# Token-major gates, output products and feed-forward blocks in a two-block layer kernel on one Trainium2 core

## The chip, the cores and the metric

The kernel runs on one core of a Trainium2 chip. The metric is the device time of one execution, in microseconds (us); a profile of one execution gives the span of the instructions beside it. Engines are named as in the profile: PE is TensorE's matmul stream, PEld its weight loads, DVE VectorE, ACT ScalarE, POOL GpSimd, SP SyncE, which issues most of the transfers.

## What is computed

Two transformer blocks, one after the other, over 256 tokens of 2048 features, all in float32. Cut to the products:

```
# block 1
mod = silu(c) @ w_ada + b_ada            # sh_m, sc_m, gt_m, sh_f, sc_f, gt_f
h = rmsnorm(x, g[0]) * (1 + sc_m) + sh_m
q, k, v, g_ret, u, gate_r, gate_s = split(h @ w_in)
y_ret = (silu(g_ret) * head_group_norm(retention(rope(q), rope(k), v))) @ w_ret_out
glu_a, glu_b = split(gelu(s5_ssm(u, ...)) @ w_s5_glu)
merged = sigmoid(gate_r) * y_ret + sigmoid(gate_s) * (glu_a * sigmoid(glu_b))
x = x + gt_m * rmsnorm(merged @ w_out, g[1])
h = rmsnorm(x, g[2]) * (1 + sc_f) + sh_f
a, b = split(h @ w_ffn_in)               # 5632 columns each
x = x + gt_f * rmsnorm((silu(a) * b) @ w_ffn_out, g[3])
# block 2
proj = rms_norm(x, norm1_w) @ w_in_2     # q k v of two attentions, conv, three merge gates
mixed = sum(sigmoid(merge_n) * (branch_n @ w_br_n) for n in 3 branches)
x = x + mixed @ w_out_2
h2 = rms_norm(x, norm2_w)
x = x + (silu(h2 @ w_ffn_gate) * (h2 @ w_ffn_up)) @ w_ffn_down
out = rms_norm(x, final_norm_w)
```

## The kernel before

**Products.** A float32 product is made of three matmuls on halves: a weight page `raw` is split into `whi` (ScalarE) and `wlo` (VectorE), an activation into a high and a low page (`hh` and `hl`, `h2h` and `h2l`, and so on), and high x high, high x low and low x high are summed in one PSUM bank. There are two forms. `gemm` (line 361) keeps a 128x128 block of weights in TensorE and moves the 256 tokens (`mm3`): the result is feature-major, features on the partitions and tokens in the row, as the next product wants its input. `gemm_tok` (line 405) keeps 128 tokens in TensorE and moves 512 columns of the weights: the result is token-major, in two banks, one for each 128 tokens. Before the change `gemm_tok` makes the values `v` and the inner gate `g_ret` of block 1 and three products of block 2; all others use `gemm`.

**The order of the work.** Products are cut into halves (`Half`): one half is 1024 weight columns of 128 rows, 24 matmuls of 256 columns or 12 of 512. `run` goes through the halves in order: it loads pages ahead on SP's queue, splits the weights of a later half (`prepare`), emits the matmuls of the present one, then its `post` (the evictions), then `pump`. Work beside the products is written as Python generators (tasks): attention, the S5 part, gating. A `yield` gives control back; its letter and number say when the task may go on: "P" from a time on TensorE's planned clock, "A" or "V" when that engine is free, with a wait in planned us. `can` and `pump` (lines 255 to 300) decide by planned costs (`Times`, `Engine`). `self.later` holds low-half subtractions that are issued a step later, by `flush`. `split_page` (435) makes an activation's two halves, the second through `later`.

**Block 1, up to its first norm.** Six passes over `w_in` (`PASSES`, `GROUPS`, line 538 on) make partial sums while the input arrives; `REST` finishes them. The gates `gate_r` and `gate_s` go through a sigmoid to DRAM (`gate_done`, 1102) and come back as `gl` pages. `ret_done` (1242) multiplies the retention branch by its gate, `glu_a` and `glu_b` (1255 to 1280) the S5 branch, with the sum split for the output product. `s5_setup` (577) makes S5's constants on GpSimd with three functions on ScalarE. `ada` sums the modulation vectors `mods` on VectorE between the weight splits; the feature-major form holds them as one column for each 128 features.

**Norms.** The output product's results are feature-major, so `y_done` (1286) and `add_done` (1753) square pages and add them up, and TensorE sums over the partitions with a column of ones (`token_sums`, `folded_sums`). `double_norm` (1313) makes two norms from three such sums and `single_norm` one; `to_columns` spreads 1/rms over the partitions by a matmul, and `keep_warm` puts matmuls of ones in between. `modulated` (492) then makes the next product's input page by page. `ffn` (1388) is used for both feed-forward blocks: pairs of gate and up blocks, `gate_up` with silu x up, and the output product through `out_gemm`.

Of the kernel before, what the change touches and what calls it, by code (L numbers as in the profile page):

```python
# [153 lines left out]
class Core:  # L154
# [250 lines left out]
    def gemm_tok(self, name, col, xs, done, kts=KT, k0=0, sums=None):  # L405

        state = []

        def emit(ks):
            def f(hi, lo):  # L410
                if not state:
                    state.extend([self.mm_bank(), self.mm_bank()])
                for n, k in enumerate(ks):
                    xh, xl = xs(k)
                    wh, wl = hi[:, 512 * n:512 * n + 512], lo[:, 512 * n:512 * n + 512]
                    for t in range(2):
                        s = slice(128 * t, 128 * t + 128)
                        mm = self.PE.matmul
                        mm(state[t], xh[:, s], wh, start=k == k0 and not sums, stop=False, skip_group_check=True)
                        mm(state[t], xl[:, s], wh, start=False, stop=False, skip_group_check=True)  # L420
                        mm(state[t], xh[:, s], wl, start=False, stop=k == kts - 1, skip_group_check=True)
            return f

        def early():
            state.extend([self.mm_bank(), self.mm_bank()])
            for b, p in zip(state, sums()):
                self.A.activation(b, p, AF.Copy)

        for k in range(k0, kts, 2):
            ks = range(k, min(k + 2, kts))  # L430
            spec = [(name, 128 * kk, slice(col, col + 512)) for kk in ks]
            post = (lambda: done(state[0], state[1])) if k + 2 >= kts else None
            self.items.append(Half(spec, emit(ks), post, early=early if sums and k == k0 else None))
# [19 lines left out]

    def folded_sums(self, accs):

        st = self.sd_bank()
        for n, acc in enumerate(accs):
            self.V.tensor_add(acc[:, :256], acc[:, :256], acc[:, 256:])
            self.token_sums(st[:, 2 * n:2 * n + 2], acc[:, :256], n == 0)
        return st  # L460

    def out_gemm(self, name, xs, done, sums, before, kts=KT, each=None):

        for i in range(8):
            c = [cols(256 * i), cols(256 * i + 128)]
            if i < 7:
                self.gemm(name, [c], xs, done(i), kts, lambda i=i: before(i))
            else:
                self.gemm(name, [c[:1], c[1:]], xs, lambda b, ps: done(7, b)(b, ps), kts, lambda: before(7), each, ends=sums)
# [22 lines left out]
    def modulated(self, x, r, A, B, name, after=None):  # L492
# [3 lines left out]
        def make(k):  # L496
# [7 lines left out]
            if after:  # L504
                after(k)
            if B is None:
                self.A.activation(hi, t, AF.Copy)
            else:
                self.A.activation(hi, t, AF.Identity, bias=B(k))

            def rest():
                if B is None:
                    self.V.tensor_sub(lo, t, hi.bitcast(F32))
                else:
                    self.V.scalar_tensor_tensor(lo, t, B(k), hi.bitcast(F32), OP.add, OP.subtract)
                done.add(k)
            self.later.append(rest)
        self_made, done = [], set()

        def more():  # L520
            make(len(self_made))
            self_made.append(1)

        def get(k):
            while len(self_made) <= min(k + (2 if k else 1), KT - 1):
                more()
# [5 lines left out]
        get.more = more  # L532
        get.make = make
        get.pairs = pairs
        get.made = self_made
# [10 lines left out]
SPLIT = 2.3  # L546
SPREAD1 = (0.0, 1.0)
# [20 lines left out]
def program(K):  # L568
# [8 lines left out]
    def s5_setup():  # L577
# [48 lines left out]
        yield "A", 0.0  # L626
# [31 lines left out]
        V.tensor_add(den, t[0], t[1])  # L658
        K.V.reciprocal(den, den)
# [112 lines left out]
    late2 = [(5, k) for k in range(16)]  # L772

    def spread(lst, a, b):
# [5 lines left out]
        for n, it in enumerate(new):  # L780
            while n % 2 == 0 and at and at[0] <= n // 2:
                at.pop(0)
                ada(*lst.pop(0))
            K.items.append(it)
# [273 lines left out]
    two = lambda c: [cols(c), cols(c + 128)]  # L1058

    def item(what, i):  # L1060
        if what == "v":
            return slice(V0 + 512 * i, V0 + 512 * i + 512)
        return {"s": lambda: two(GS0 + 256 * i), "u": lambda: two(U0 + 256 * i), "q": lambda: rope_cols(Q0, i), "k": lambda: rope_cols(K0, i),
                "r": lambda: two(GR0 + 256 * i)}[what]()
# [11 lines left out]
    def ready(it, src):  # L1076
# [13 lines left out]
        elif what in "rs":  # L1090
            gate_done("rs".index(what), i)(0, src[0])
# [10 lines left out]
    def gate_done(which, i):  # L1102
        def f(b, ps):
            p = K.page("gate")
            A.activation(p, ps, AF.Sigmoid)
            K.G.dma_start(gsp[8 * which + i], p)
# [8 lines left out]
    def one_pass(group, k0, k1, more, then=None):  # L1115
# [3 lines left out]
        def emit(k, its):  # L1119
            def f(hi, lo):  # L1120
                if not banks:
                    held.extend(K.sd_bank() for _ in range(8 - MM))
                    pool = [K.mm_bank() for _ in range(MM)] + held
                    for what, i in group:
                        banks[what, i] = [pool.pop(0) for _ in range(2 if what == "v" else 1)]
                xh, xl = h(k)
                at = 0
                for it in its:
                    if it[0] == "v":
# [26 lines left out]
        for k in range(k0, k1):  # L1156
            for n in range(2):
                its, w = [], 0
                for it in group:
                    size = 512 if it[0] == "v" else 256  # L1160
# [41 lines left out]
    for g, k0 in REST:  # L1202
        for it in groups[g]:
            if it[0] == "v":
                K.gemm_tok("w_in", V0 + 512 * it[1], h, lambda a, b, it=it: ready(it, [a, b]), k0=k0, sums=lambda it=it: added(it))
# [4 lines left out]
    def g_done(hp):  # L1210
        def f(a, b):
            tg = [K.page("tg"), K.page("tg")]
            for t, p in enumerate((a, b)):
# [5 lines left out]
    for n in range(16):  # L1219
        if ("rs"[n // 8], n % 8) not in planned:  # L1220
            K.gemm("w_in", [two(GR0 + 256 * n)], h, gate_done(n // 8, n % 8))
    for hp in range(4):
        K.gemm_tok("w_in", R0_ + 512 * hp, h, g_done(hp))
# [9 lines left out]
    def ret_before(i):  # L1233
        def f():
            if i == 0:
# [3 lines left out]
            gate_load(i + 1)  # L1239
        return f  # L1240

    def ret_done(i):
        def f(b, ps):
            merged[i] = gl.pop(i)
            V.tensor_mul(merged[i], ps, merged[i])
        return f
    xrf = lambda k: K.halves_of(xr)(k)
    for i in range(8):
        K.gemm("w_ret_out", [[cols(256 * i), cols(256 * i + 128)]], xrf, ret_done(i), before=ret_before(i))


    mg = {}

    def glu_before(i):
        def f():
            if i == 0:
                K.finish(G["s5"])
                K.finish(G["ys"])
            gate_load(8 + i)
            gate_load(9 + i)  # L1260
        return f
    hold = {}

    def glu_a(i):
        def f(b, ps):
            hold[i] = ps
        return f

    def glu_b(i):
        def f(b, ps):  # L1270
            sg = K.page("sg")
            A.activation(sg, ps, AF.Sigmoid)
            V.tensor_mul(sg, hold.pop(i), sg)
            V.tensor_mul(sg, sg, gl.pop(8 + i))
            V.tensor_add(sg, sg, merged.pop(i))
            mg[i] = K.split_page(sg, "mg")
        return f
    ysf = lambda k: K.halves_of(ys)(k)
    for i in range(8):
        K.gemm("w_s5_glu", [[cols(256 * i), cols(256 * i + 128)]], ysf, glu_a(i), kts=8, before=glu_before(i))  # L1280
        K.gemm("w_s5_glu", [[cols(D + 256 * i), cols(D + 256 * i + 128)]], ysf, glu_b(i), kts=8)


    up = {}

    def y_done(i, mod, last, half=None):
        w = slice(0, 512) if half is None else slice(256 * half, 256 * half + 256)

        def f(b, ps):
            u = up[i] = up.get(i) or K.page("u")  # L1290
            x = G["xl"][i]
            if i == 0:
                G["acc"] = new = [K.page("acc") for _ in range(3)]
            else:
                new = [K.page("sq") for _ in range(3)]
            sy, sx, su = new
            A.activation(sy[:, w], ps[:, :w.stop - w.start], AF.Square)
            for j in range(2) if half is None else [half]:
                s = slice(256 * j, 256 * j + 256)
                A.activation(u[:, s], ps[:, s.start - w.start:s.stop - w.start], AF.Copy, scale=mods[:, 16 * mod + 2 * i + j:][:, :1])  # L1300
            A.activation(su[:, w], u[:, w], AF.Square)
            V.tensor_mul(sx[:, w], x[:, w], u[:, w])
            if half == 1:
                last([p[:, w] for p in new])
            elif i:
                for acc, p in zip(G["acc"], new):
                    V.tensor_add(acc[:, w], acc[:, w], p[:, w])
        return f

    def y_sums():  # L1310
        G["st"] = K.folded_sums(G.pop("acc"))

    def double_norm(A_, B_, dst, name, new):

        st = G.pop("st")
        st2 = K.sd_bank()
        for n, sq in enumerate(new):
# [627 lines left out]
```

## Time and profile before

| | |
|---|---|
| median of 3 runs | 3415.16 us (3412.63 to 3415.56) |
| the profiled execution: time | 3421.82 us |
| the profiled execution: span | 3420.0 us |
| granted TensorE clock, mean | 0.995 |
| weight and other data read from HBM | 716.32 MB, 214 GB/s over the span |
| weight splits, ScalarE and VectorE | 1,124 each, of 128x1024 |

A busy time of the page is the sum over an engine's instructions, and a share of it is of the span. A line of the timeline gives the start of an instruction and how long its record lasts; matmuls are pipelined, so the time that one costs is the distance from its start to the next start (its pitch), and not the length of its record. "[0.53 <-DVE wlo]" means that the engine stood idle for 0.53 us before and that the tile `wlo`, written by VectorE, released it. Nearly every instruction has line 150, a helper that records all operations, so instructions are told apart by the names of their tiles.

### The profile page before, as it was taken

Reading aid. Unit: us, or ns where it says so; the run is one execution under the profiler, and the core shown is the slowest. Engines: PE = TensorE matmul, PEld = TensorE weight load, DVE = VectorE, ACT = ScalarE, POOL = GpSimd, SP = SyncE. Lnnn points to the kernel's source line nnn. Section 1 sums busy time; section 2 is a strip of 40 time slices with the busy share of each in tenths; the row PEclk is TensorE's granted clock in tenths of the full one; section 3 lists DMA queues with packets and bytes.
Section 4 is the critical chain, followed back from the end, with each engine's and each line's share of the span. In section 5 each row is a group of like instructions: output and inputs, shape, how many; then the busy total and the mean of one; then the engine's idle time right before and its main releaser. Section 6 shows DMA issues by size and latency. Waiting matters only on the chain.

```text
span 3420.0 us, 63152 instructions
## 1 busy us (share of the span) xinstructions
PE 3378.1 (99%) x27336; PEld 3291.6 (96%) x27336; DVE 2038.9 (60%) x2376; ACT 1542.6 (45%) x1906; POOL 171.3 (5%) x309
## 2 busy tenths in 40 slices
PE   8899999999999999999999999999999999999999
PEld 7889998999999999999988999999999999999998
DVE  7787889778765555445555455444555644444444
ACT  4456555444444444444455444433444444444343
POOL 3401221000000000000000000000000000000000
PEclk9999999999999999999999999999999999999999
DMA  8786777788665665555554444555555545455543
GB/s 330 288 307 245 254 254 265 282 304 313 229 227 214 219 237 216 200 191 190 192 195 177 175 172 178 189 181 185 185 201 193 193 177 186 184 178 195 204 181 118
DMA packets 118745, 735.76 MB, mean 215 GB/s; under 512 B 15345, under 2 KB 18945, under 8 KB 34369
## 3 DMA queue, kind: packets, MB, share of 16 engines
q1 hardware_dynamic: 110050, 716.19, 57.5%
q0 software_dynamic: 7840, 14.48, 1.3%
q8 instruction: 214, 3.51, 0.4%
q10 hardware_dynamic: 576, 1.05, 0.1%
q14 instruction: 65, 0.53, 0.0%
HBM read 716.32 MB, written 14.68 MB: 214 GB/s over the span
## 4 chain that ended last, share of the span: by engine, by line
PE 93%; DVE 2%; DMA 2%; POOL 1%; ACT 1%; issue 0%; SPq 0%; DVEq 0%; ACTq 0%
PE mmb L150 89%; PE sdb L150 4%; POOL s5x L150 1%; DMA raw<-ws 1%; DVE raw L150 1%; DVE wlo L150 1%; ACT whi L150 0%; DMA s5x<-s5p 0%; DMA xl<-xT 0%; DMA s5b<-s5bc 0%; DVE xl L150 0%; ACT part L150 0%; DVE mt L150 0%; DVE part L150 0%; DVE rt L150 0%
## 5 line engine op out<-in xcount | busy, mean ns | idle before, releaser
L150 DVE TENSOR_TENSOR wlo<-raw,whi 128x1024 fp32r<-128x1024 f32 x1124 | 1358.9, 1222 | 654.9 <-ACT whi L150 652.1
L150 ACT ACTIVATE whi<-raw 128x1024 fp32r<-128x1024 f32 x1124 | 1178.4, 1057 | 1238.6 <-PE mmb L150 1089.2
L150 PE MATMUL mmb<-hh,whi 128*128 128x256 f32 x2148 | 612.5, 285 | 1.2 <-ACT part L150 1.1
L150 PE MATMUL mmb<-hl,whi 128*128 128x256 f32 x2148 | 609.0, 284 | 0.0
L150 PE MATMUL mmb<-hh,wlo 128*128 128x256 f32 x2148 | 608.8, 283 | 0.0
L150 PE MATMUL mmb<-h3h,whi 128*128 128x256 f32 x1552 | 442.3, 285 | 1.0 <-ACT h3h L150 1.0
L150 PE MATMUL mmb<-h3l,whi 128*128 128x256 f32 x1552 | 439.4, 283 | 0.3 <-DVE h3l L150 0.2
L150 PE MATMUL mmb<-h3h,wlo 128*128 128x256 f32 x1552 | 439.2, 283 | 0.0
L150 PEld LDWEIGHTS mmb<-hh,whi 128*128 128x128 f32 x2148 | 413.6, 193 | 5.0 <-ACT part L150 1.3
L150 PEld LDWEIGHTS mmb<-hl,whi 128*128 128x128 f32 x2148 | 413.6, 193 | 1.2
L150 PEld LDWEIGHTS mmb<-hh,wlo 128*128 128x128 f32 x2148 | 413.3, 192 | 0.0
L150 PE MATMUL mmb<-h2h,whi 128*128 128x256 f32 x1408 | 398.6, 283 | 1.1 <-ACT h2h L150 1.1
L150 PE MATMUL mmb<-h2l,whi 128*128 128x256 f32 x1408 | 398.7, 283 | 0.5 <-DVE h2l L150 0.4
L150 PE MATMUL mmb<-h4l,whi 128*128 128x256 f32 x1408 | 398.6, 283 | 0.1
L150 PE MATMUL mmb<-h4h,whi 128*128 128x256 f32 x1408 | 398.6, 283 | 0.0
L150 PE MATMUL mmb<-h4h,wlo 128*128 128x256 f32 x1408 | 398.5, 283 | 0.0
L150 PE MATMUL mmb<-h2h,wlo 128*128 128x256 f32 x1408 | 398.5, 283 | 0.0
L150 PEld LDWEIGHTS mmb<-h3h,whi 128*128 128x128 f32 x1552 | 297.8, 192 | 3.2 <-issue 1.4
L150 PEld LDWEIGHTS mmb<-h3l,whi 128*128 128x128 f32 x1552 | 297.9, 192 | 0.9 <-DVE h3l L150 0.7
L150 PEld LDWEIGHTS mmb<-h3h,wlo 128*128 128x128 f32 x1552 | 297.8, 192 | 0.0
L150 PEld LDWEIGHTS mmb<-h2h,whi 128*128 128x128 f32 x1408 | 270.3, 192 | 1.3 <-ACT h2h L150 1.3
L150 PEld LDWEIGHTS mmb<-h2l,whi 128*128 128x128 f32 x1408 | 270.3, 192 | 0.9 <-DVE h2l L150 0.9
(324 smaller groups left out, 5788.0 us busy)
## 6 DMA issues: line engine op xcount, KB each, us to landing
raw<-ws SPq DMA_DIRECT2D x657, 1024.0 KB, 4.9
gsp<-gate POOLq DMA_DIRECT2D x16, 256.0 KB, 4.6
gl<-gsp SPq DMA_DIRECT2D x16, 256.0 KB, 7.3
xl<-x1d SPq DMA_DIRECT2D x16, 256.0 KB, 6.4
x<-xT SPq DMA_DIRECT2D x8, 256.0 KB, 6.4
xl<-xT SPq DMA_DIRECT2D x8, 256.0 KB, 9.1
x1d<-u POOLq DMA_DIRECT2D x8, 256.0 KB, 2.5
x2d<-u POOLq DMA_DIRECT2D x8, 256.0 KB, 2.6
```

The costliest lines, as they stand in the source:

```text
L150: return f(*args, **kw)
```

## The change

Gates, the retention, S5 and branch outputs, the output projections, and both feed-forward blocks now use `gemm_tok`: tokens stationary, 512 weight columns moving. What follows each of them is token-major:

- `untok` (new) turns a token-major pair of pages back: per half page four 128x128 transposes on TensorE into a free bank, then `split_page` from the bank. `turned` makes the next product finish that task before it reads the page.
- `gate_done`, `ret_done`, `glu_b`, `glu_a`, `merge_done`, `br_done`, `gate`/`gate_up` work on two pages of 128 tokens x 512 features.
- The sums of the norms come from `accum_out` of the squaring instruction, in [128, 1] columns; `reduce_sum` adds the four. `token_sums` in the stream, `folded_sums` and `to_columns` leave these norms. `TAIL` = 30 and 16 matmuls of ones are put in front of a norm. `normed` (new) scales the pages per token, turns them with transposes and applies gain and shift per feature on the way out of the bank.
- Gains that vary along the row are needed as rows: GpSimd writes two of the modulation vectors to DRAM (`rows`), and SP loads each as broadcast pages `gb` (`load_rows`); `final_norm_w` comes as pages `fw`. The residual of block 1 is loaded token-major from a new input `xt`; the output is written token-major.
- `s5_setup` waits 60 planned us before its ScalarE functions and 40 before its reciprocal. `GROUPS[1]` holds the gate columns as ("r", 0), ("r", 1) of 512.

```diff
+    def untok(self, pages, ident, dst, n, name):
+        yield "P", 0.0
+        for half in range(2):
+            b, = yield from self.sd(1)
+            for vb in range(2):
+                for t in range(2):
+                    at = 256 * half + 128 * vb
+                    self.PE.transpose(b[:, 256 * vb + 128 * t:256 * vb + 128 * t + 128], pages[t][:, at:at + 128], ident)
+            yield "A", 0.0
+            dst[2 * n + half] = self.split_page(b, name)
+            self.later.append(lambda b=b: self.sd_free(b))
+            yield "P", 0.0
+TAIL = (30, 16)
...
-        yield "A", 0.0
+        yield "A", 60.0
         A.activation(ab, th, AF.Abs)
...
+        yield "V", 40.0
         K.V.reciprocal(den, den)
...
+    def glu_a(n):
+        def f(g, banks):
+            for t, ps in enumerate(banks):
+                sg = sgs[n][t]
+                V.tensor_mul(sg, ps, sg)
+            for t in range(2):
+                sg = sgs[n][t]
+                V.tensor_mul(sg, sg, gl.pop(8 + 2 * n + t))
+                V.tensor_add(sg, sg, merged.pop((n, t)))
+            mgt[n] = K.start("un", K.untok(sgs.pop(n), ident, mg, n, "mg"))
         return f
...
+            for t, ps in enumerate(banks):
+                A.activation(K.page("junk"), ps, AF.Square, accum_out=sm[:, t, n:n + 1])
+                V.tensor_mul(us[t], ps, G["gb"][n])
+            for t in range(2):
+                A.activation(K.page("junk"), us[t], AF.Square, accum_out=sm[:, 2 + t, n:n + 1])
+                V.scalar_tensor_tensor(K.page("junk"), us[t], 1.0, G["xl"][2 * n + t], OP.mult, OP.mult,
+                                       accum_out=sm[:, 4 + t, n:n + 1])
...
         def gate_up(j):
-            def f(b, ps):
-                st = K.page("fst")
-                s, t = st[:, :256], st[:, 256:]
-                A.activation(s, ps[:, :256], AF.Silu)
-                V.tensor_mul(t, s, ps[:, 256:])
-                if j % 2 == 0:
-                    hid[j // 2] = (K.page("hh", F32R), K.page("hl", F32R))
-                sl = slice(256 * (j % 2), 256 * (j % 2) + 256)
-                hi, lo = hid[j // 2]
-                A.activation(hi[:, sl], t, AF.Copy)
-                K.later.append(lambda: V.tensor_sub(lo[:, sl], t, hi[:, sl].bitcast(F32)))
+            def f(g, banks):
+                for s, ps in zip(st[j], banks):
+                    V.tensor_mul(s, ps, s)
+                tasks[j] = K.start("un", K.untok(st.pop(j), K.ident, hid, j, "h"))
             return f
...
+        K.gemm_tok([(wa, ca), (wb, cb)], xs, lambda g, banks: (gate_up if g else gate)(0)(g, banks))
+        for j in range(1, FB // 4):
+            K.gemm_tok([(wa, ca + 512 * j)], xs, gate(j))
+            K.gemm_tok([(wb, cb + 512 * j)], xs, gate_up(j))
+        out_tok(wo, lambda k: K.turned(hid, tasks)(k), done, before, FB, each)
```

**The order of the instructions.** In the instruction lists, 20,736 of the 24,240 weight matmuls of 256 columns become 10,368 of 512; 336 transposes of 128x128 are added. The rows below are of those lists; a wait is on the count of the engine or queue named.

TensorE in the first feed-forward block, before the change: a half's matmuls follow one another from one block of features to the next (`h2h`, `h2l` are the normed input).

```order
L150 MATMUL mmb<-h2h,wlo 128x256
L150 MATMUL mmb<-h2h,whi 128x256 [waits Activation_49]
L150 MATMUL mmb<-h2l,whi 128x256
L150 MATMUL mmb<-h2h,wlo 128x256 [waits DVE_49]
L150 MATMUL mmb<-h2h,whi 128x256
```

The same place after the change, at the end of a product of gate and up columns; `fst` is silu(gate) x up.

```order
L150 MATMUL mmb<-whi,h2h 128x512
L150 MATMUL mmb<-whi,h2l 128x512
L150 MATMUL mmb<-wlo,h2h 128x512
L150 MATMUL sdb<-ident,fst 128x128 [waits DVE_49] x2
L150 MATMUL sdb<-ident,fst 128x128 x2
L150 MATMUL mmb<-whi,h2h 128x512 [waits Activation_49]
L150 MATMUL mmb<-whi,h2l 128x512
```

The first four transposes stand directly behind the product's last matmul and wait for VectorE; the next product's matmuls stand behind them.

VectorE at the gated sum in front of the first output product, before (`sg` is the sigmoid, then the sum; `gl` the gate's page).

```order
L150 TENSOR_TENSOR wlo<-raw,whi 128x1024 [waits PE_49,Activation_49]
L150 TENSOR_TENSOR wlo<-raw,whi 128x1024 [waits DMAHW0_49,PE_49,Activation_49]
L150 TENSOR_TENSOR sg<-mmb,sg 128x512 [waits Activation_49]
L150 TENSOR_TENSOR sg<-sg,gl 128x512 [waits DMAHW6_49,DVE_49]
L150 TENSOR_TENSOR sg<-sg,gl 128x512 [waits DVE_49]
L150 TENSOR_TENSOR wlo<-raw,whi 128x1024 [waits PE_49]
L150 TENSOR_TENSOR mgl<-sg,mgh 128x512 [waits Activation_49]
```

And after, where `mgl` is subtracted from the bank of the transposes (`sdb`).

```order
L150 TENSOR_TENSOR wlo<-raw,whi 128x1024 [waits PE_49,Activation_49]
L150 TENSOR_TENSOR wlo<-raw,whi 128x1024 [waits DMAHW6_49,PE_49,Activation_49]
L150 TENSOR_TENSOR sg<-mmb,sg 128x512 [waits PE_49] x2
L150 TENSOR_TENSOR sg<-sg,gl 128x512 [waits DMAHW3_49,DVE_49]
L150 TENSOR_TENSOR sg<-sg,gl 128x512 [waits DVE_49]
L150 TENSOR_TENSOR sg<-sg,gl 128x512 [waits DMAHW4_49]
L150 TENSOR_TENSOR sg<-sg,gl 128x512 [waits DVE_49]
L150 TENSOR_TENSOR wlo<-raw,whi 128x1024 [waits Activation_49]
L150 TENSOR_TENSOR wlo<-raw,whi 128x1024 [waits DMAHW7_49,Activation_49]
L150 TENSOR_TENSOR mgl<-sdb,mgh 128x512 [waits Activation_49]
```

Three operations on one page became six on two pages, and two weight splits stand between them and the low part.

ScalarE at the set-up of the S5 part (`s5x`), in the passes over `w_in`, before; 20 splits `whi` stand ahead of this place in the list.

```order
L150 ACTIVATE whi<-raw 128x1024 x2
L150 ACTIVATE s5x<-s5x 128x32
L150 ACT_TABLE_LOAD
L150 ACTIVATE s5x<-s5x 128x32
L150 ACTIVATE s5x<-s5x,cst 128x32
L150 ACTIVATE whi<-raw 128x1024
L150 ACTIVATE part<-mmb 128x512 x5
```

After, 40 splits stand ahead of it.

```order
L150 ACTIVATE part<-mmb 128x512 x5
L150 ACTIVATE part<-sdb 128x512 x3
L150 ACTIVATE whi<-raw 128x1024 x3
L150 ACTIVATE hh<-mt,mods 128x256
L150 ACTIVATE whi<-raw 128x1024 x4
L150 ACTIVATE s5x<-s5x 128x32
L150 ACT_TABLE_LOAD
L150 ACTIVATE s5x<-s5x 128x32
L150 ACTIVATE s5x<-s5x,cst 128x32
```

The three functions moved behind the next evictions of partial sums (`part`).

## Rows read from the trace of the kernel before

**Rows 1.** The page: busy time of each engine, share of the span, instructions.

```profile
PE 3378.1 (99%) x27336; PEld 3291.6 (96%) x27336; DVE 2038.9 (60%) x2376; ACT 1542.6 (45%) x1906; POOL 171.3 (5%) x309
```

**Rows 2.** The chain of waits: start and length in us, what ran.

```profile
2646.90 759.74 PE mmb L150 x6329
```

**Rows 3.** Timeline of PE: wide matmuls around four transposes (start, length, instruction).

```profile
548.80 0.39 PE L150 MATMUL mmb<-wlo,hh 128*128 128x512 f32 x1
549.03 0.60 PE L150 MATMUL sdb<-ident,tg 128*128 128x128 f32 x4
...
549.70 0.40 PE L150 MATMUL mmb<-whi,hl 128*128 128x512 f32 x1
...
552.02 0.39 PE L150 MATMUL mmb<-wlo,hh 128*128 128x512 f32 x1
...
554.08 0.39 PE L150 MATMUL mmb<-whi,hh 128*128 128x512 f32 x1
...
560.65 0.39 PE L150 MATMUL mmb<-wlo,hh 128*128 128x512 f32 x1
```

**Rows 4.** Timeline of all engines at the end of a wide product of block 2.

```profile
1760.14 1.23 DVE L150 TENSOR_TENSOR wlo<-raw,whi 128x1024 fp32r<-128x1024 f32 x1 [1.50 <-ACT whi L150]
...
1761.31 1.28 ACT L150 ACTIVATE vg<-mmb 128x512 f32<-128x512 f32 x2 [1.21 <-PE mmb L150]
...
1761.57 0.39 PE L150 MATMUL mmb<-wlo,h3h 128*128 128x512 f32 x1
```

**Rows 5.** Groups by form (busy, mean ns); the chain; VectorE's timeline.

```profile
L150 DVE TENSOR_TENSOR sg<-mmb,sg 128x512 f32<-128x512 f32 x8 | 5.5, 691 | 16.6 <-ACT sg L150 16.6
L150 ACT ACTIVATE sq<-u 128x512 f32<-128x512 f32 x12 | 7.6, 633 | 0.4
...
L150 DVE SCALAR_TENSOR_TENSOR raw<-raw,cact 128x2048 f32<-128x2048 f32 x96 | 219.7, 2289 | 6.9 <-DMA raw<-ws 6.7
...
3409.41 0.27 ACT rs L150
...
3411.18 4.87 DVE L150 TENSOR_TENSOR xl<-xl,sdb 128x512 f32<-128x512 f32 x8 [0.85 <-PE sdb L150]
```

**Rows 6.** Timeline of PE in the first passes; last row: 40 to 52 us, columns as in Rows 8.

```profile
33.44 0.50 PE L150 MATMUL mmb<-wlo,hh 128*128 128x512 f32 x1 [0.53 <-DVE wlo L150]
33.77 0.39 PE L150 MATMUL mmb<-whi,hh 128*128 128x512 f32 x1
34.00 0.39 PE L150 MATMUL mmb<-whi,hl 128*128 128x512 f32 x1
...
43.99 0.80 PE L150 MATMUL mmb<-whi,hh 128*128 128x512 f32 x1 [4.33 <-ACT part L150]
...
46.72 0.41 PE L150 MATMUL mmb<-hh,whi 128*128 128x256 f32 x1
...
48.21 0.37 PE L150 MATMUL mmb<-hl,whi 128*128 128x256 f32 x1
...
40.00:52.00 12.00, 8.01 (x38) 7.12 (x39) 9.21 (x12) 8.25 (x13) 0.00 (x0) 0.72 0.96 338
```

**Rows 7.** Timeline of PE at the end of the first output product.

```profile
898.34 1.50 PE L150 MATMUL sdb<-ones,acc 128*128 128x1 f32 x12
...
900.38 0.28 PE L150 MATMUL mmb<-mgh,wlo 128*128 128x256 f32 x1
...
913.08 0.38 PE L150 MATMUL mmb<-h2l,whi 128*128 128x256 f32 x1
```

**Rows 8.** S5 set-up: ScalarE's timeline, TensorE's waits (total, times, longest), engines in 88:100.

```profile
94.65 0.23 ACT L150 ACTIVATE s5x<-s5x 128x32 f32<-128x32 f32 x1 [13.14 <-POOL s5x L150]
...
PE mmb L150 <- ACT part L150: 16.8, 4, 10.6
...
88.00:100.00 12.00, 1.89 (x5) 1.50 (x6) 2.39 (x2) 5.32 (x11) 9.57 (x33) 0.70 0.38 146
```

In the last row: length, busy us (and count) of PE, PEld, DVE, ACT and POOL, mean granted clock, DMA share, GB/s.

**Rows 9.** The same columns for 500 to 600 us.

```profile
500.00:600.00 100.00, 100.00 (x801) 85.22 (x800) 95.03 (x122) 54.12 (x68) 18.52 (x40) 1.00 0.78 275
```

More of the change, by code (lines that the diff above doesn't have):

```diff
@@ L417, in f @@
                         s = slice(128 * t, 128 * t + 128)
[L418 to L421, printed above, removed]
+                        mm, b = self.PE.matmul, state[g][t]
+                        mm(b, xh[:, s], wh, start=k == k0 and not sums, stop=False, skip_group_check=True)
@@ L503, in make, with get @@
             self.V.scalar_tensor_tensor(t, src, A(k), r, OP.mult, OP.mult)
[L504 to L511, printed above, removed]
+            self.A.activation(hi, t, AF.Identity, bias=B(k))
+            self.later.append(lambda: self.V.scalar_tensor_tensor(lo, t, B(k), hi.bitcast(F32), OP.add, OP.subtract))
+        def get(k):
+            raise NotImplementedError
@@ new lines, in modulated, with normed, prep, turn @@
+        get.make = make
+        get.pairs = pairs
+        get.made = []
+        return get
+    def normed(self, z, ident, A, B, name, after=None):
+        pairs, zs, done = {}, {}, set()
+        def prep(n):
+            if n < 4 and n not in zs:
+                zs[n] = z(n)
+        def turn(n, half):
+            if n > 3 or 2 * n + half in pairs:
+                return
+            prep(n)
+            i = 2 * n + half
+            pair = pairs[i] = (self.page(name + "h", F32R), self.page(name + "l", F32R))
+            b = self.sd_bank()
+            for vb in range(2):
+                for t in range(2):
+                    at = 256 * half + 128 * vb
+                    self.PE.transpose(b[:, 256 * vb + 128 * t:256 * vb + 128 * t + 128], zs[n][t][:, at:at + 128], ident)
+            for vb in range(2):
+                k, s = 2 * i + vb, slice(256 * vb, 256 * vb + 256)
+                hi, lo = (p[:, s] for p in pair)
@@ L512, in rest @@
                 if B is None:
-                    self.V.tensor_sub(lo, t, hi.bitcast(F32))
+                    self.A.activation(hi, b[:, s], AF.Copy, scale=A(k))
                 else:
[L515 to L522, printed above, removed]
-        def get(k):
-            while len(self_made) <= min(k + (2 if k else 1), KT - 1):
-                more()
+                    t = self.page("mt")[:, :256]
@@ new lines, in turn @@
+                self.later.append(rest)
+            if i == 7 and after:
+                after()
+        def get(k):
+            n = k // 4
+            if k == 0:
+                prep(0)
+                turn(0, 0)
+                prep(1)
+                turn(0, 1)
+            elif k not in done and k // 2 not in pairs:
+                turn(n, k // 2 % 2)
+            if k % 4 == 0:
+                prep(n + 1)
+            if k % 4 == 2:
+                turn(n + 1, 0)
+            if k % 4 == 3:
+                turn(n + 1, 1)
@@ L772, in program @@
     late2 = [(5, k) for k in range(16)]
+    ready_rows = lambda part, k: (lambda: rows(part)) if k == 15 and part in (2, 5) else None
     def spread(lst, a, b):
@@ L1124, in f @@
                     for what, i in group:
[L1125 removed]
+                        banks[what, i] = [pool.pop(0) for _ in range(2 if what in TOK else 1)]
                 xh, xl = h(k)
@@ L1262, in program @@
[L1262 to L1266, printed above, removed]
-        return f
[L1269 to L1276, printed above, removed]
+            for i in range(4):
+                gate_load(8 + 2 * n + i)
+        return f
@@ L1277, in glu_b @@
         return f
     ysf = lambda k: K.halves_of(ys)(k)
-    for i in range(8):
-        K.gemm("w_s5_glu", [[cols(256 * i), cols(256 * i + 128)]], ysf, glu_a(i), kts=8, before=glu_before(i))
-        K.gemm("w_s5_glu", [[cols(D + 256 * i), cols(D + 256 * i + 128)]], ysf, glu_b(i), kts=8)
+    for n in range(4):
+        K.gemm_tok([("w_s5_glu", D + 512 * n)], ysf, glu_b(n), kts=8, before=glu_before(n))
+        K.gemm_tok([("w_s5_glu", 512 * n)], ysf, glu_a(n), kts=8)
     up = {}
[L1286 to L1307, printed above, removed]
-        return f
@@ new lines, in program, with out_tok, w_before @@
+    mgf = lambda k: K.turned(mg, mgt)(k)
+    def out_tok(name, xs, done, before, kts=KT, each=None):
+        for n in range(4):
+            K.gemm_tok([(name, 512 * n)], xs, done(n), kts, before=lambda n=n: before(n), each=each if n == 3 else None)
+    def w_before(n):
+        if n == 0:
+            reload("xl", xsrc)
+            for i in range(4):
+                load_rows(2, i)
+        if n == 3:
+            K.sqrt_soon()
+    out_tok("w_out", mgf, lambda n: y_done(n, mid), w_before)
@@ L1799, in end2, with z @@
[L1799 to L1807 removed]
+        def z(n):
+            out = [K.page("z"), K.page("z")]
+            for t in range(2):
+                A.activation(out[t], xl[2 * n + t], AF.Copy, scale=r[:, t:t + 1])
+            return out
```

464 lines of the change are left out of this document (248 added, 216 removed), and 2 rows, old and new, of the table GROUPS.

## The prediction

> **What bounds the kernel now.** I read the page first: TensorE is busy for 3378 of 3420 us [rows 1], so only its own work can shorten the run by much; VectorE, at 60%, matters where TensorE waits for it. Then the chain of waits: one unbroken piece of it is the whole second feed-forward block, 6,329 matmuls in 759.74 us and no wait [rows 2]. That gives the price of a narrow matmul (256 tokens moving): 759.74 / 6329 = 120.0 ns. The timeline gives the price of a wide one (512 weight columns moving) from the token-major products that the kernel has already: 29 pitches between 554.08 and 560.65 us, 226.6 ns each [rows 3]. Two narrow ones take 240.1. The difference, 13.5 ns, is what the change is about.
>
> **The change part by part.** Sums are against the profiled execution (3421.8 us, span 3420.0); its own time is 6.6 us above the median of the runs, 3415.2, and I take the same difference off the median.
>
> *Narrow to wide.* The order lists hold 24,240 narrow weight matmuls before and 3,504 after, 1,344 wide ones before and 11,712 after: 20,736 narrow become 10,368 wide. 20,736 x 0.1200 = 2,489 us becomes 10,368 x 0.2266 = 2,349 us: **-140 us**, all on the path, as nothing else bounds a stretch like [rows 2].
>
> The Trainium skill, page "TensorE: Matmul & The Clock Gate", section "Back-to-back issue gap", speaks against this: a matmul costs its columns at 2.4 GHz and only about 2.5 ns more, so a pair of narrow ones would take 218.4 ns beside 215.8 and the whole exchange would give some 27 us. The rows disagree with it (120.0 and 226.6 ns are 13.3 ns above the columns in both widths), and the measurement decides.
>
> *Transposes.* Results now come out token-major, but the next product wants features on partitions: 336 transposes of 128x128 are added (176 for the two feed-forward blocks, 96 for the three norms, 32 each for the two merged inputs of the output projections), in 84 fours. The trace has such fours: from the wide matmul at 548.80 to the second one behind the four, at 549.70, 0.90 us instead of 0.453, so 0.445 for a four; and the next ten matmuls run at 232 instead of 226.6 ns, 0.05 more [rows 3]. Six fours lie in the norms' tails, 78 in the stream: 78 x 0.495 = **+39 us**.
>
> *Waits of the transposes.* `untok` gives control back once before its first transpose, without a time to wait for, so the planner lets it run at once. The order list shows what comes of it: in all 30 uses the first four stands directly behind the last matmul of the product whose result it turns, and TensorE, which takes its work in order, stands still until VectorE has made that result. A wide product's first bank can be read 0.26 us before its last matmul starts (the eviction at 1761.31 beside the matmul at 1761.57), and VectorE gets out of the weight split before it 0.20 us before that start (1760.14 + 1.23 = 1761.37) [rows 4]. A 128x512 product takes 0.69 us; eight behind one another without dependence take 4.87, 0.61 each [rows 5]. With the last matmul's start as zero:
> - feed-forward, 22 times: two products, the second from its bank's end, 0.42, to 1.11; second transpose at 1.2 instead of 0.34: 0.86 us each, 18.9.
> - gated sum in front of the first output projection, 4 times: six operations, two of them behind their predecessor's result, end at 3.8; 3.56 each, 14.2.
> - mixed sum of the second block, 4 times: four operations end at 2.37; 2.13 each, 8.5.
>
> Together **+42 us**. Below, it cannot go under 0; above, one stop in three with a modulation product of 2.29 us in front of it [rows 5] would add 23. I take the middle value, since in the list the weight splits in front of these products are done in time and most modulation products stand behind them.
>
> *The clock after a stop.* In the trace, a stop of 4.33 us at 43.99 is followed by six wide matmuls in 2.73 us (1.36 at full speed) and seven narrow ones in 1.49 (0.84): 2.0 us lost, at half of 2.4 GHz, and the stretch's mean granted clock is 0.72. A shorter stop, 0.53 at 33.44, is followed by the full pitch, 0.23 us at 33.77 [rows 6]. The 0.86 us stops are nearer to the short one, so I count them free of it. The three norms that have a restart behind them now stand still for some 4 us after their 30 or 16 warming matmuls, and two of the eight longer stops may catch it: 5 x 2.0 = **+10 us** (0 to 22).
>
> *Norm tails.* Now 12.7 us lie between the last matmul of an output projection (900.38) and the steady stream after it (913.08), and about the same at the second [rows 7]. The new double norm: four squares on ScalarE at 0.63, taken as 0.72 with the read of the sum, and VectorE's last product, 3.5; eight tiny operations at 0.3, as the 0.27 of a root, 2.4; four products at 0.61; one weight split of 1.2 that stands in front; 0.45 for the low part: 10.1. That is -2.6 twice [rows 5, 7]. The single norm gets +1 (two products and two squares where there was half a page); the one at the end, 0. The 12 column-sum matmuls inside the stream (1.5 us, twice) go [rows 7]. Together **-7 us** (-15 to +5).
>
> *The set-up of the S5 part.* ScalarE now waits 13.14 us for GpSimd at 94.65, with weight splits and partial sums queued behind it, and TensorE stands still for 10.6 us [rows 8]. The change puts a 60 us delay in front: the order list has the same operation 20 weight splits later, by when GpSimd is long done. The transfers idled in that stop (DMA share 0.38) and were near their limit before, so I count **-10 us** (-13 to -3). The 40 us delay before the reciprocal costs nothing; its reader stands further back.
>
> *The rest.* Eight 256 KB rows of gains and four more rows are loaded on SP's queue in front of weights, GpSimd writes the gains out in 4-byte pieces, and around 500 to 600 us VectorE is 95% busy [rows 9], so that a faster TensorE may find it late: **+8 us** (0 to 26).
>
> Sum: -140 + 39 + 42 + 10 - 7 - 10 + 8 = -58, rounded up for the second decimals to -59: 3363 for the profiled execution, **3356 us** for the median.
>
> **The rivals.**
> - *The stops are mostly hidden.* If the first multiplication ran earlier than I think, the 42 us and 4 of the clock's 10 go: 3310. For it: VectorE is idle for 40% of the time. Against: the product cannot start before its bank is complete [rows 4].
> - *The first block up to its norm keeps its time.* 3,840 of the narrow matmuls lie before 900 us; their 26 us are lost if VectorE or the weight stream is the bound there: 3382. For it: 95% VectorE [rows 9]. Against: TensorE is at 100% in the same row.
> - *The wide matmul runs at 232 ns everywhere*, as it does behind each interruption [rows 3]: 10,368 x 5.4 ns = 56 us back, 3412. Against: the full pitch returns after ten matmuls.
> - *The clock falls at every stop* (the slower side). A granted clock of 0.70 over 12 us makes a low stretch of 12 x 0.30 / 0.5 = 7.2 us [rows 8]; the stop itself, 1 to 3.6 us, lies in it, and half of the rest, 2 to 3 us, is lost each time. It decides from 2.3 us a stop, where 30 of them take the 59 us and the 10 already counted for it; at 3.0 the time is 3356 - 10 + 30 x 3.0 = 3436. For it: the stops of 4.33 and 10.6 us were both followed by half speed. Against: the full pitch behind a stop of 0.53 us [rows 6].
> - *The fixed cost per matmul is not there in the new places.* If the 13.3 ns belong to the narrow products' addresses and not to each instruction, the pair saves 2.6 ns and 113 us of the gain go: 3469. The rule quoted above would have it so; against it stand both pitches [rows 2, 3].
>
> **How the numbers follow.** My forecast 0.55 (own range 3332 to 3380); stops hidden 0.12; first block keeps its time 0.18; 232 ns everywhere 0.06; clock 0.07; no fixed cost 0.02. The range 3312 to 3402 leaves out the last three and part of the second, about 0.2. About 0.2% (7 us) is what a measurement tells from no change: faster 0.55 + 0.12 + 0.18 and half of 0.06 is 0.88, same 0.03, slower 0.09.
>
> **What would show it.** In the profile after: wide pitch 226.6 ns in the feed-forward stretches, each some 20 us shorter between its norms; TensorE's row of waits led by the transposes of `fst`, `sg` and `sig` waiting for VectorE, 0.9, 3.6 and 2.1 us each; no wait for `s5x`; half-speed pitches only behind the norms. A share of TensorE's stops well over 80 us, or half-speed pitches behind `fst`, would prove me wrong, as would a wide pitch over 230.

## The result and the profile after

The change takes 3355.12 us (median of 4 runs, 3354.22 to 3357.32) against 3415.36 us before: a ratio of 0.9826, 95% interval 0.9809 to 0.9843, or 60 us less. The forecast was 3356 us. The sum came out right, in part because errors cancelled: of its terms the norm tails were mis-sized, the clock's stood in the wrong place, and the S5 set-up gave more than was counted.

The page of the changed kernel, busy time of each engine (answers to [rows 1]): TensorE has 63 us of idle time where it had 42, and is busy for 89 us less.

```profile
PE 3289.2 (98%) x17276; PEld 2773.6 (83%) x17276; DVE 1994.5 (59%) x2192; ACT 1541.8 (46%) x1852; POOL 196.8 (6%) x311
```

The chain of waits, its last unbroken piece in the second feed-forward block (answers to [rows 2]): 236.01 us for 1041 matmuls are 226.7 ns each, the wide pitch of [rows 3], in a place that was narrow before.

```profile
3104.23 236.01 PE mmb L150 x1041
```

What TensorE waited for (total, times, longest): the three tiles that the forecast named lead the list, and the wait for the partial sums, 16.8 us in [rows 8] with 10.6 of it at the S5 set-up, is 4.5.

```profile
PE sdb L150 <- DVE sg L150: 12.5, 8, 2.2
PE sdb L150 <- DVE fst L150: 9.2, 24, 0.8
PE sdb L150 <- DVE sig L150: 6.7, 8, 1.5
PE mmb L150 <- ACT part L150: 4.5, 2, 3.3
```

One product's end in the first feed-forward block, in the timeline: the first transpose starts 1.23 us behind the last matmul, when VectorE has the first page, the other three when it has the second. From the last matmul (945.05) to the second one behind the four (947.49) it takes 2.44 us, where two pitches are 0.45. The second four (from 950.02) has no wait.

```profile
943.61 1.28 ACT L150 ACT_TABLE_LOAD   x1
...
944.90 1.08 ACT L150 ACTIVATE fst<-mmb 128x512 f32<-128x512 f32 x2
945.05 0.39 PE L150 MATMUL mmb<-wlo,h2h 128*128 128x512 f32 x1
945.53 1.29 DVE L150 TENSOR_TENSOR fst<-mmb,fst 128x512 f32<-128x512 f32 x2 [3.40 <-ACT fst L150]
...
946.28 0.33 PE L150 MATMUL sdb<-ident,fst 128*128 128x128 f32 x1 [0.84 <-DVE fst L150]
...
946.88 0.55 PE L150 MATMUL sdb<-ident,fst 128*128 128x128 f32 x3 [0.27 <-DVE fst L150]
947.18 0.48 PE L150 MATMUL mmb<-whi,h2h 128*128 128x512 f32 x1
...
947.49 0.39 PE L150 MATMUL mmb<-whi,h2l 128*128 128x512 f32 x1
...
950.02 0.60 PE L150 MATMUL sdb<-ident,fst 128*128 128x128 f32 x4
...
950.70 0.39 PE L150 MATMUL mmb<-whi,h2l 128*128 128x512 f32 x1
```

That is the first of the block's eleven, where ScalarE had to load a function table first (943.61). In the others the second matmul behind the four comes 1.34 us later than two pitches alone would bring it; a four without a wait makes that 0.45 us, so that 0.89 us are the stop. The gated sum stops TensorE longer, and here half speed follows. Its timeline from 713.03 on: 3.99 us beyond the two pitches (713.03 to 717.48), three pitches at full speed, then pitches of 0.42 to 0.43 us instead of 0.227, which is 1.2 GHz instead of 2.4.

```profile
713.03 0.39 PE L150 MATMUL mmb<-wlo,ysh 128*128 128x512 f32 x1
...
714.07 2.74 DVE L150 TENSOR_TENSOR sg<-sg,gl 128x512 f32<-128x512 f32 x4
715.53 0.33 PE L150 MATMUL sdb<-ident,sg 128*128 128x128 f32 x1 [2.11 <-DVE sg L150]
...
716.86 0.55 PE L150 MATMUL sdb<-ident,sg 128*128 128x128 f32 x3 [1.00 <-DVE sg L150]
...
717.48 0.39 PE L150 MATMUL mmb<-whi,ysl 128*128 128x512 f32 x1
...
719.02 0.63 PE L150 MATMUL mmb<-whi,ysh 128*128 128x512 f32 x1
719.45 0.63 PE L150 MATMUL mmb<-whi,ysl 128*128 128x512 f32 x1
```

The windows of this place, of the first norm and of one mixed sum (columns as in [rows 8]: the third number from the end is the granted clock) show 0.93 and 0.94 at the two sums, and 1.00 at the norm, behind which the forecast had looked for half speed.

```profile
710.00:735.00 25.00, 21.89 (x94) 17.49 (x93) 16.67 (x19) 9.60 (x11) 0.00 (x0) 0.93 0.72 262
...
880.00:905.00 25.00, 24.24 (x142) 20.77 (x141) 14.52 (x27) 15.40 (x28) 2.20 (x4) 1.00 0.55 205
2420.00:2450.00 30.00, 28.34 (x121) 22.88 (x121) 15.17 (x16) 11.27 (x12) 0.00 (x0) 0.94 0.45 160
```

By stage, from the first matmul of one input to that of the next, with the kernel before taken from its second profile (below): up to the first output product 803.7 to 800.9 us; that product and its norm 103.4 to 97.6; first feed-forward block and norm 771.6 to 750.5; block 2 up to its output product 862.0 to 856.4; that product 97.1 to 92.5; second feed-forward block up to its last matmul 765.5 to 746.2. The two feed-forward blocks give 40 of the 60 us. Block 2's middle, where 3,456 narrow matmuls became 1,728 wide (23 us), gives only 6: the fours of `sig` and of the norm, the `sig` stops and half speed behind two of them take the rest.

### The profile page after: what moved, and what is told of

It is laid out like the page before. It is cut to its first block, busy times and chain, and to the rows that moved or that the text cites. A ratio compares the mean times of both kernels' runs of the same rounds, so it can differ in the third digit from the quotient of the medians.

```text
span 3352.1 us, 42924 instructions
## 1 busy us (share of the span) xinstructions
PE 3289.2 (98%) x17276; PEld 2773.6 (83%) x17276; DVE 1994.5 (59%) x2192; ACT 1541.8 (46%) x1852; POOL 196.8 (6%) x311
## 4 chain that ended last, share of the span: by engine, by line
PE 89%; DVE 5%; DMA 3%; ACT 1%; issue 1%; SPq 0%; DVEq 0%; ACTq 0%
PE mmb L150 85%; PE sdb L150 4%; DMA raw<-ws 2%; DVE raw L150 1%; DVE wlo L150 1%; DVE fst L150 1%; ACT whi L150 1%; DVE sg L150 0%; ACT part L150 0%; DVE part L150 0%; DMA s5b<-s5bc 0%; DVE sig L150 0%; DVE t L150 0%; DVE u L150 0%; DVE xl L150 0%
## 5 line engine op out<-in xcount | busy, mean ns | idle before, releaser
L150 PE MATMUL mmb<-whi,hh 128*128 128x512 f32 x1169 | 463.1, 396 | 8.8 <-ACT part L150 4.5
L150 PE MATMUL mmb<-wlo,hh 128*128 128x512 f32 x1169 | 457.7, 392 | 2.8 <-DVE wlo L150 2.8
L150 PE MATMUL mmb<-whi,hl 128*128 128x512 f32 x1169 | 457.2, 391 | 0.0
L150 PE MATMUL mmb<-whi,h2h 128*128 128x512 f32 x704 | 276.5, 393 | 0.7 <-ACT h2h L150 0.7
L150 PE MATMUL mmb<-whi,h4h 128*128 128x512 f32 x704 | 276.5, 393 | 0.1
L150 PE MATMUL mmb<-whi,h4l 128*128 128x512 f32 x704 | 274.1, 389 | 0.4 <-DVE h4l L150 0.4
L150 PE MATMUL mmb<-wlo,h4h 128*128 128x512 f32 x704 | 274.3, 390 | 0.0
L150 PE MATMUL mmb<-wlo,h2h 128*128 128x512 f32 x704 | 274.3, 390 | 0.0
L150 PE MATMUL mmb<-whi,h2l 128*128 128x512 f32 x704 | 274.2, 389 | 0.0
L150 PE MATMUL mmb<-whi,h3h 128*128 128x512 f32 x576 | 227.5, 395 | 0.0
```

Of the source, the lines that this page charges most:

```text
L150: return f(*args, **kw)
```

## The experiments

**The changed kernel again**, as the measure for runs made beside it.

> The changed kernel unaltered, as the measure for the other runs of this call. Every theory: 3355 us, 60 us below the kernel before. In its profile the 30 first fours of transposes with their waits cost 1.3 us each for fst, 4.0 to 4.5 for sg, 2.5 for sig, and half-speed pitches stand behind the sg and sig stops.

Measured 3356.13 us, kernel before 3413.34. All four `sg` and three of the four `sig` stops have half speed behind them this time, two in the first profile: which of the `sig` stops is followed by it changes from run to run.

**Transposes when their pages are made.** In `untok`:

```diff
-        yield "P", 0.0
+        self.times.mark = max(t for p in pages for _, _, t, _ in self.times.span(p)[0][0])
+        yield "P", 0.0
```

> untok waits for the planned end of its input pages before the first transpose, so that the transposes stand one or two halves behind the product. Theory (the stops are on the path and nothing else takes their place): the 20.9 us behind fst, 15 behind sg and 8.6 behind sig go, with the 7.8 us of half speed behind the sg and sig stops: 3355 - 52 = 3303 us. Rival 1 (VectorE is late anyway, and the stop comes back at the transposes' new place or at the next product): within 5 us of 3355. Rival 2 (the stops go but the half speed has another cause): 3311, with half-speed pitches where they were.

Measured 3310.52 us, 45.6 less than the changed kernel beside it. All 60 fours now take 0.45 us, and no half speed is left behind them. The first four of the gated sum, with 0.90 us from the last matmul to the second one behind it:

```profile
718.89 0.39 PE L150 MATMUL mmb<-wlo,ysh 128*128 128x512 f32 x1
719.12 0.60 PE L150 MATMUL sdb<-ident,sg 128*128 128x128 f32 x4
...
719.79 0.40 PE L150 MATMUL mmb<-whi,ysl 128*128 128x512 f32 x1
```

So the stops, 44.1 us of them, were on the path, and rival 1 falls. But 7 of the 52 us came back as one new wait, in the first output product: the time is the one that rival 2 gave, without the cause that it gave. The row of waits, and SP's timeline ahead of it:

```profile
PE mmb L150 <- DVE wlo L150: 6.0, 4, 4.8
```

```profile
787.71 1.72 SPq L131 DMA_DIRECT2D raw<-ws  x2
789.48 7.59 SPq L131 DMA_DIRECT2D xl<-xt  x8
797.36 3.90 SPq L131 DMA_DIRECT2D gb<-grow  x4
801.64 16.54 SPq L131 DMA_DIRECT2D raw<-ws  x6
```

Then VectorE's and TensorE's timelines, ten us later:

```profile
808.95 2.29 DVE L150 SCALAR_TENSOR_TENSOR raw<-raw,cact 128x2048 f32<-128x2048 f32 x1 [9.85 <-DMA raw<-ws]
```

```profile
807.53 0.39 PE L150 MATMUL mmb<-whi,mgl 128*128 128x512 f32 x1
812.69 0.80 PE L150 MATMUL mmb<-wlo,mgh 128*128 128x512 f32 x1 [4.78 <-DVE wlo L150]
813.29 0.63 PE L150 MATMUL mmb<-whi,mgh 128*128 128x512 f32 x1
```

VectorE is named, but it stood idle for 9.85 us itself, released by `raw<-ws`: the weights were late, behind twelve loads of 256 KB that SP issued in one go.

**The loads a quarter at a time**, on top of that, and alone in the changed kernel:

```diff
-        if n == 0:
-            reload("xl", xsrc)
-            for i in range(4):
-                load_rows(2, i)
+        for m in ((0, 1) if n == 0 else (n + 1,)):
+            if m < 4:
+                load_x("xl", xsrc, 2 * m)
+                load_x("xl", xsrc, 2 * m + 1)
+                load_rows(2, m)
```

> turn_made, and the twelve pages that y_done needs in the first output product (eight of the residual, four rows of gains, 3 MB) are loaded a quarter at a time, one product ahead, instead of all in front of its weights. Theory (in turn_made the weights behind these 3 MB came late, and TensorE stood still for 4.8 us with 2.2 us of half speed behind it): both go, 3310.5 - 7 = 3304 us. Rival (the stream of weights is late there in any case, by its sum of bytes): the stop moves to a later half, within 3 us of 3310.

> The changed kernel with the spread loads alone, the transposes where they were. Theory (behind the stops of the gated sum TensorE is late enough that the weights are there in time): no difference, 3356 us within 3. Rival (the loads cost the changed kernel something as well, as part of the 8 us counted for the rest): 3349 to 3353 us.

Measured 3303.51 us with both (ratio to before 0.9672, interval 0.9658 to 0.9685) and 3354.81 alone. So the new wait was the loads', and the 52 us of the stops are all to be had; in the changed kernel itself the loads cost nothing that can be told from the noise. The version with both beats the changed kernel by 52 us and the kernel before by 112.

**Matmuls of ones in the stops.** Before the first transpose of `mg` and `mx`:

```diff
+            if half == 0 and name != "h":
+                self.keep_warm(b[:, :128], 10 if name == "mg" else 6)
```

> In the stops behind the gated sum and the mixed sum TensorE runs 10 and 6 matmuls of ones (0.23 us each) in front of the transposes; the stops stay as long as they are. Theory (half speed follows because TensorE stood still for 2 to 3.5 us): no half-speed pitch behind sg and sig, 3355 - 7.8 + 1 = 3348 us. Rival (the half speed there is not due to TensorE's idling): half-speed pitches stay, 3355 to 3357 us.

Measured 3347.86 us, 8.3 less than the changed kernel beside it. The stops are as long as before (4.0 and 2.55 us beyond two pitches) and no half-speed pitch stands behind them: the half speed follows TensorE's idling and cost some 8 us. The second stop of the gated sum (each of the ten matmuls of ones makes two records), with pitches of 0.22 and 0.23 us behind it:

```profile
742.21 2.40 PE L150 MATMUL sdb<-ones 128*128 128x128 f32 x20
...
745.81 0.55 PE L150 MATMUL sdb<-ident,sg 128*128 128x128 f32 x3 [1.00 <-DVE sg L150]
...
746.43 0.39 PE L150 MATMUL mmb<-whi,ysl 128*128 128x512 f32 x1
746.65 0.39 PE L150 MATMUL mmb<-wlo,ysh 128*128 128x512 f32 x1
746.88 0.39 PE L150 MATMUL mmb<-whi,ysh 128*128 128x512 f32 x1
```

**Norms without matmuls of ones.** `TAIL = (30, 16)` becomes `(0, 0)`.

> The changed kernel without the matmuls of ones in front of its norms (TAIL = (0, 0)); TensorE then stands still for about 8 us at the two double norms and 5 us at the two single ones. Theory (half speed follows because TensorE stood still): half speed behind the three norms that have a product behind them, 1.4 to 2.0 us each as behind the other long stops, and slower transposes there: 3356 + 6 = 3362 us. Rival (the half speed comes back to something else than idling, and the matmuls of ones do nothing): 3356 us within 2, or less.

Measured 3362.97 us, 7 more than the 3356 of the changed kernel (5 to 6 by the ratios to before: 0.9845, interval 0.9832 to 0.9858, beside 0.983 and 0.9826). At the first norm, the timeline of TensorE:

```profile
896.88 0.47 PE L150 MATMUL sdb<-ident,z 128*128 128x128 f32 x1 [6.24 <-ACT z L150]
...
899.54 0.80 PE L150 MATMUL mmb<-whi,h2h 128*128 128x512 f32 x1 [0.25 <-ACT h2h L150]
...
900.59 0.63 PE L150 MATMUL mmb<-wlo,h2h 128*128 128x512 f32 x1
901.02 0.63 PE L150 MATMUL mmb<-whi,h2h 128*128 128x512 f32 x1
```

Pitches of 0.43 us: with the 30 and 16 matmuls no half speed follows the norms, without them it stands behind all three, for 1.3, 0.7 and 2.1 us, and the tails themselves take 0.24 to 0.48 us longer.

**The S5 set-up**, both ways: without its two delays in the changed kernel, and with nothing but them in the kernel before.

```diff
-        yield "A", 60.0
+        yield "A", 0.0
...
-        yield "V", 40.0
         K.V.reciprocal(den, den)
```

> Both delays of the S5 set-up are taken out of the changed kernel. Theory (ScalarE's wait for GpSimd held up weight splits and stopped TensorE for 10.6 us, with 1.9 us of half speed behind it): 10 to 12 us more, 3365 to 3367, with a stop of some 10 us near 90 us. Rival (the stream of weights bounds the first 200 us, so that a stop there is made good later): within 3 us of 3355 although the stop is seen.

> The kernel before with nothing changed but the two delays of the S5 set-up. Theory (the 10.6 us stop and the 1.9 us of half speed behind it go, and the run without the delays in the changed kernel lost 12.6 us): 3413 - 12 = 3401 us. Rival (in the kernel before the stream of weights bounds the first passes more closely, so that part is given back): 3405 to 3413 us.

Measured 3368.73 us without them, 12.6 more than the changed kernel beside it, and 3402.0 with them in the kernel before (ratio 0.9957, interval 0.9943 to 0.9971, so 10 to 19 us less than the runs beside it). The stop is back where it was in [rows 8]:

```profile
95.17 0.80 PE L150 MATMUL mmb<-whi,hh 128*128 128x512 f32 x1 [10.71 <-ACT part L150]
95.77 0.63 PE L150 MATMUL mmb<-whi,hl 128*128 128x512 f32 x1
```

Nothing was made good by the transfers; the half speed behind the stop comes on top. Both delays were taken out or put in together, so what the second one does by itself is not shown.

**Wide matmuls issued as two narrow ones**, with the same stationary tokens:

```diff
+                        for c in (slice(0, 256), slice(256, 512)):
+                            b = state[g][t][:, c]
+                            mm(b, xh[:, s], wh[:, c], ...)
+                            mm(b, xl[:, s], wh[:, c], ...)
+                            mm(b, xh[:, s], wl[:, c], ...)
```

> In the changed kernel 11,304 of the 11,712 wide matmuls are issued as two of 256 columns each, with the same stationary tokens; all else stays. Theory (what the change gains is one fixed cost of 13 ns a matmul, whichever operand stands still): a pitch of 120.0 ns, 11,304 x 13.5 ns = 153 us more, 3356 + 153 = 3509 us. Rival 1 (the gain is due to what stands still, tokens or weights): a pitch near 113.3 ns, 3356 us. Rival 2 (a fixed cost of 2.5 ns a matmul, and the rest of the narrow pitch comes from weights standing still): 11,304 x 2.5 = 28 us more, 3384 us.

Measured 3495.85 us, 140 more than the 3356 of the changed kernel (ratio to before 1.0226, interval 1.0212 to 1.024). In the second feed-forward block the timeline has 25 pitches in 3.00 us, 120.0 ns:

```profile
2749.83 0.28 PE L150 MATMUL mmb<-wlo,h4h 128*128 128x256 f32 x1
...
2752.83 0.28 PE L150 MATMUL mmb<-whi,h4h 128*128 128x256 f32 x1
```

So what the change gains is a cost of each matmul, 13.3 ns above its 256 columns at 2.4 GHz (120.0 - 106.7), and not which operand stands still; rivals 1 and 2 fall. Each matmul brings a weight load with it, the halves too, and this run does not take the two apart. Of the 13 us that are missing from the 153, 7 were given back in the first 820 us, which grew by 17.6 us where the matmuls there took 25 more.

**Every four of transposes twice**, `for vb in range(2)` as `for vb in (0, 1, 0, 1)`.

> In the changed kernel each four of transposes of untok is issued twice into the same bank, 60 fours more. Theory (a four costs TensorE its four transposes, 0.44 us, on the path and beside the stops): 60 x 0.44 = 26 us more, 3382 us. Rival 1 (most of the 0.45 us is the change between products and transposes, paid once for a group): under 10 us more, under 3366 us. Rival 2 (the transposes are hidden in the stops that stand in front of half of them): 30 x 0.44 = 13 us more, 3369 us.

Measured 3382.56 us, 27 more than the changed kernel's 3356, by the ratios to before (0.9895, interval 0.9882 to 0.9909, beside 0.9826) some 23. Eight transposes in the stream take 0.88 us, four 0.45, and behind the `fst` stops too the eight cost 0.43 more: the cost is the transposes' own.

**The kernel before, once more.**

> The kernel before once more, for a second profile: its first one took 3421.8 us, 6.6 above the median of its runs. Theory (the difference lies in the first 200 us, where transfers are near their limit): everything behind the first feed-forward block's start has the same length as in the first profile within 1 us, and the time of 3411 to 3416 us comes with a shorter stretch up to there. Rival (it is spread over the whole run, as by a clock): all stretches are shorter alike, by 0.2%.

Its profile: 3413.36 us, span 3411.6. Neither theory nor rival was right. Up to the first output product it is 2.6 us shorter, the stretches with the first and the second double norm are 2.8 and 3.1 us shorter, and behind the second norm nothing differs. In the first profile the earlier part of both double norms, with half of its matmuls of ones, ran at half speed (granted clock 0.79 from 897 to 913 us), in the second it did not (1.00). TensorE in the middle of the first norm, first profile:

```profile
906.10 3.57 PE L150 MATMUL sdb<-ones 128*128 128x128 f32 x20
```

and second:

```profile
901.87 2.40 PE L150 MATMUL sdb<-ones 128*128 128x128 f32 x20
```

This tail takes 12.46 us beyond two pitches in the one, 9.38 in the other, and the second norm's differs as much. Six of the 8.5 us between the two spans lie there.

## Why the prediction was right, term by term

Against the second profile of the kernel before, the span fell by 3411.6 - 3352.1 = 59.5 us.

- *Narrow to wide, -140.* Right: -139, with both pitches seen in their new and old places, and the cause shown by the split. The Trainium skill's small cost of a matmul (page "TensorE: Matmul & The Clock Gate", section "Back-to-back issue gap") does not hold for these products: it gives 2.5 ns beside the columns, for a matmul by itself, where both traces show 13.3 in a stream with a weight load at each matmul; the section itself says that in such a stream both set the spacing. The rival of 3469 us, no fixed cost in the new places, is out, and so is the one of 232 ns everywhere: the pitch is 226.7.
- *Transposes, +39.* 37 by the profile: 78 fours at 0.45, and some 2 us of slower pitches behind them. The slower pitches were counted too high (0.05 us a four, measured 0.03), the fours rightly.
- *Waits of the transposes, +42.* Right in size and place: 20.8 us behind `fst` (forecast 18.9), 14.9 behind `sg` (14.2), 8.4 behind `sig` (8.5), 44.1 in all, and shown by the run that moved the transposes. The rival that they are hidden is out, as the runs took its price, 3310, only when the stops were removed.
- *The clock, +10.* Near in size by luck, wrong in place. The step that failed is "two of the eight longer stops may catch it", with the norms as the likelier place: none of the three norms had half speed behind it, where the run without the 30 and 16 matmuls of ones has it behind all three, and six of the eight longer stops had it. Set beside the same stretches without it, these lose 8.6 us in all, and the run with ones in the stops got 8.3 back. Over the five runs of the changed kernel with the stops left as they are and no ones in them (first, again, without the delays, spread loads, no tail) it followed 18 of 20 `sg` stops of 3.5 us, 11 of 20 `sig` stops of 2.1, and none of the 110 `fst` stops, most of them of 0.89 us.
- *Norm tails, -7.* The term was mis-sized. The -2.6 for each double norm was taken from a profile in which these tails ran at half speed for a part. Against the second profile they fall from 9.38 and 9.23 to 8.96 and 9.06, -0.6 together; with the column sums gone (-2.8), +0.7 for the single norm and its sums (-0.5) it is -3.2.
- *The set-up, -10.* Slightly low: -12.6 by taking the delays out. The stop is 10.7 us long, and the half speed behind it was not counted; that the transfers, near their limit, would take some of it back did not come true.
- *The rest, +8.* By difference 59.5 = 139 - 37 - 44.1 - 8.6 + 3.2 + 12.6 - rest, so about +6. It lies ahead of the first output product: by the terms above that stretch should be some 11 us shorter and is 2.8, while the other stages come out within 1 us. So the rival that the first block keeps its time was right for a part of its 26 us. The loads in front of the first output product have no part in it. What the trace has there is more waiting of TensorE for VectorE's tiles: 9.6 us for `qk`, `tg`, `xrl` and `wlo`, where the second profile of the kernel before has 3.4 (7.2 in the second profile of the changed kernel). That fits the forecast's reason, a VectorE that is found late, but no run took these waits out, so it is not shown. Two rows of the changed kernel:

```profile
PE sdb L150 <- DVE qk L150: 2.7, 1, 2.7
PE sdb L150 <- DVE xrl L150: 2.4, 1, 2.4
```

and of the kernel before, in its second profile, which has none for `xrl`:

```profile
PE sdb L150 <- DVE qk L150: 1.3, 1, 1.3
```

Taking the profiled run's 6.6 us over the median off both kernels was wrong as well: it was no property of the kernel, and the sum against the profiled execution (-59, 3363) was 9 us off the 3354.2 of the changed kernel's own profiled run. The median came right by luck: the real terms, with less from the tails and more from the set-up than was counted, happen to add up to the same -59 from a profile at the median.

## What to carry to other kernels

A matmul has a cost beside its columns; where the same sum can be done with 512 moving columns instead of 256, take the pitch of both from the trace and multiply, and then price the transposes that the new orientation needs, here a quarter of the gain. An instruction that needs another engine's result belongs one step behind the work that can go on without it: a hand-back to the planner with no time to wait for puts it in front, and here that cost more (52 us) than the transposes themselves (37). Before the sum is made against one profile, look whether its tails run at the clock that another profile has.

## What the runs showed of the hardware

Half speed behind stops of 2.1 us came and went from run to run, and matmuls of ones inside the stops prevented it in all eight of the run that had them, at no cost where the stop was there anyway. A stop that names VectorE can be a transfer's: removing 44.1 us of stops let TensorE reach weights that lay behind 3 MB of other loads, and 7 us of the gain waited there until the loads were spread.
